# Hybrid SSD/RWKV block: gate and up with tokens on the output partitions

## The chip, the cores and the metric

The kernel runs on one core of a Trainium2 chip, in fp32. Matrix products are made of three float32r matmuls each (high part by high part, high by low, low by high), so that they come near to fp32. The metric is the device time of one execution in microseconds, the median of several runs.

## The reference

The block takes x, 256 tokens by 2048 channels. A normalised copy goes through one input projection into two mixers (a Mamba-2 state space mixer and an RWKV-7 time mixer), whose outputs go through w_out and are added to x. Then comes the feed-forward part, which the change touches, and a last norm:

```python
h = h + jnp.concatenate([y_ssd, y_rwkv], axis=-1) @ w_out[l]
v = rms_norm(h, norm2_g[l])
h = h + (jax.nn.silu(v @ w_gate[l]) * (v @ w_up[l])) @ w_down[l]
return rms_norm(h, norm_f_g)
```

w_gate and w_up are 2048 x 5632, w_down is 5632 x 2048, all fp32: 138 MB, read once.

## The kernel before

**Streamed weights.** Every weight matrix is read in units of 0.5 MB, in the order of use, on the queue of SyncE, into a ring of four buffers (raw). ScalarE casts a unit to its high part whi (L192), VectorE subtracts to get the low part wlo (L193); both have rings of four. TensorE consumes a unit with 24 matmuls of 256 columns or 12 of 512.

**Two forms of product.** gemm_a (L267) keeps a 128x128 piece of the weights stationary and moves the 256 tokens of one row tile of the activations: the output has channels on the partitions and tokens along the free dimension. A unit is four row tiles of 256 columns. gemm_b (L283) keeps 128 tokens of an activation tile stationary and moves 512 weight columns: the output has tokens on the partitions, in two tiles of one PSUM bank each (tokens 0 to 127, and 128 to 255). A unit is two row tiles of 512 columns. The input projection uses gemm_a, but for its z columns; z uses gemm_b (L1021), and so do w_out and w_down through add_out (L304), which adds the result to h. All product tiles come from a pool of four PSUM banks (mm), tiles for transposes and small work from another of four (mx).

**The second norm.** uh and ul (high and low part) hold h times the norm's weight with channels on the partitions, 16 row tiles. They are made by to_channels (L234) from PE transposes of h, a quarter of the channels after each quarter of the last w_out product. The rows' factor, one over the root mean square of each token, is left out there and comes in later: row_scale (L217) makes R, which holds it along the free dimension on every partition (a product of ones with a diagonal matrix), and scaled (L229) multiplies a product with it in PSUM, on VectorE.

**Feed-forward.** The loop (L1054) goes over 11 blocks of 512 feed-forward columns. In each, two halves of 256 columns have a gate and an up product by gemm_a (w_gate, silu on ScalarE, w_up, multiplication on VectorE), and the result is split into ah and al, with channels on the partitions, as the w_down product needs it. The w_down product of a block is traced after gate and up of the next block (prev). The last 256 rows of w_down are a piece of their own with the last norm, one half of the tokens after the other.

**Order.** The queues are in the order of the program but for small shifts that the scheduler of the language makes. side is a list of small pieces with due ticks; every unit of a product is one tick, and side.at(t, f) has f traced at the t-th tick from then. In the feed-forward part of the kernel before nothing is in it.

Of the kernel before, what the change touches and what calls it, by code (L numbers as in the profile page):

```python
# [10 lines left out]
F32 = mybir.dt.float32  # L11
# [20 lines left out]

# ticks of a window at which the parts of three pairs of blocks are traced
PREP = (1.081, 1.2, 4.2, 5.2, 5.536, 6.756, 8.05, 9.2)
# [7 lines left out]
class Side:  # L42
    """Work of the mixers, cut into small pieces that are traced between the pieces of the dense products."""

# [24 lines left out]
def tile_hybrid_block(ctx: ExitStack, tc: tile.TileContext, x, norm1_g, w_in, conv_w, conv_b, dt_bias, A_log, D_skip,  # L69
# [26 lines left out]

# [1 line left out]
    h = big.tile([P, 2, D], F32, name="h")  # L98
# [11 lines left out]
    eps6 = constcol(1e-6, "eps6")  # L110
    # products that nothing reads: the tensor engine has its full clock only after a busy stretch
    ps = mxt("ps_up")
# [31 lines left out]

# [1 line left out]
    trimask = const.tile([P, P], F32, name="trimask")  # L146
# [12 lines left out]
    for s in range(2):  # L159
        for hh in range(2):  # L160
            a = hh * 64
            nc.vector.tensor_tensor(sel[:, s, a + 32 * s:a + 32 * s + 32], ident[:, a:a + 32], ident[:, a + 32:a + 64],
                                    ALU.add)
    # msk16: lower off-diagonal blocks on the way from 16 to 32 ([t, c])
    bmask = const.tile([P, 4], F32, name="bmask")
# [21 lines left out]
    colC = const.tile([P, 96], F32, name="colC")  # L187
# [1 line left out]
    def split(raw, order=lambda ins: ins):  # L189
# [10 lines left out]
    def square(i, pool, b, n, eng, order=lambda ins: ins):  # L200
        """the sum of squares of a quarter of each row"""
        src = h[:, b, n * 512:(n + 1) * 512]
        acc = ssq[i][:, b, n:n + 1]
        if eng == "act":
            order(nc.scalar.activation(pool.tile([P, 512], F32, name="sq_a"), src, AF.Square, accum_out=acc))
        else:
            order(nc.vector.scalar_tensor_tensor(pool.tile([P, 512], F32, name="sq_v"), src, 1.0, src, ALU.mult,
                                                 ALU.mult, accum_out=acc))
# [8 lines left out]
    def row_scale(i, pool):  # L217
        """one over the root mean square of each token, along the free dimension of every partition"""
        nonlocal R
        ps = mxt("ps_R")  # L220
        for b in range(2):
            r = finish(i, b)
            dg = pool.tile([P, P], F32, name="diag_r")
            nc.vector.tensor_scalar(dg, ident, r, None, ALU.mult)
            nc.tensor.matmul(ps[:, b * P:(b + 1) * P], ones, dg, start=True, stop=True)
        R = const.tile([P, T], F32, name="R")
        nc.scalar.copy(R, ps[:, :T])

    def scaled(ps):  # L229
        """a product of the raw rows becomes the one of the normalised rows"""  # L230
        nc.vector.tensor_tensor(ps, ps, R.unsqueeze(1).broadcast_to([P, 2, T]), ALU.mult)
        return ps

    def to_channels(n, gcol, order=lambda ins: ins):  # L234
        """a quarter of h times the norm's weight, with channels on the partitions; the rows' scale comes later"""
        nonlocal uh, ul
        if n == 0:
            uh = big.tile([P, KT, T], F32R, name="uh")
            ul = big.tile([P, KT, T], F32R, name="ul")
        tiles = []  # L240
        for k2 in range(2):
            ps = mxt("ps_n").rearrange("p (a t) -> p a t", a=2)
            tiles.append(ps)
            for b in range(2):
                for j in range(2):
                    c = n * 512 + (2 * k2 + j) * P
                    order(nc.tensor.transpose(out=ps[:, j, b * P:(b + 1) * P], in_=h[:, b, c:c + P], identity=ident))

        def half(k2):
            ks = [(4 * n + 2 * k2 + j, tiles[k2][:, j]) for j in range(2)]  # L250
            for k, ps in ks:
                order(nc.scalar.activation(uh[:, k], ps, AF.Copy, scale=gcol[:, k:k + 1]))
            for k, ps in ks:
                order(nc.vector.scalar_tensor_tensor(ul[:, k], ps, gcol[:, k:k + 1], uh[:, k].bitcast(F32), ALU.mult,
                                                     ALU.subtract))

        return half

    def load_a(w, cols, k0):
        """four row tiles of 256 columns; cols: [(place, width, column)]"""  # L260
        raw = wpool.tile([P, 4, 256], F32, name="raw", tag="raw", bufs=4)
        wv = w.rearrange("(k p) c -> p k c", p=P)
        for at, n, c in cols:
            nc.sync.dma_start(out=raw[:, :, at:at + n], in_=wv[:, k0:k0 + 4, c:c + n])
        return raw
# [17 lines left out]
    def gemm_b(w, r0, c0, acts, name):  # L283
        """acts: [(hi, lo)] with [P, T] each, one for a row tile of w; 512 columns"""
        ps = [mmt(name).rearrange("p a t -> p (a t)") for _ in range(2)]
# [18 lines left out]
    def add_out(w, r0, ys, then=None):  # L304
        """ys: [(hi, lo)] of two row tiles each"""
        acts = [(yh[:, k], yl[:, k]) for yh, yl in ys for k in range(2)]
# [7 lines left out]

    # the first product starts while x and its weights still come in, a quarter of the channels after the other
    pin = tc.keep_in_program_order
# [62 lines left out]

# [1 line left out]
    dtb = ssdc.tile([P, 3, 32], F32, name="dtb")  # L381
# [50 lines left out]

# [1 line left out]
    yq = deque()  # L434
    NCH = 8

    def rwkv_pair(pi, st):
# [119 lines left out]
        def swap(dst, src, tmp):  # L557
            """the 64x64 blocks of src [(h c), (b c t)] transposed into dst [(h t), b c, c]"""
            fl = src.rearrange("p a t -> p (a t)")
# [35 lines left out]

        # inverse of (I - N): blocks of 16 on one partition each, by halves of halves
        def inv_out():
# [15 lines left out]
        def inv_level(s):  # L613
            def f():
# [3 lines left out]
                def blocks(t, at, swap):  # L618
                    """block (row offset or column offset) of each of the nm diagonal blocks, [nm, s, s]"""
                    v = t[:, :nm * 34 * s].rearrange("p (m x) -> p m x", m=nm)[:, :, at:at + 16 * s]  # L620
                    v = v.rearrange("p m (j t) -> p m j t", t=16)[:, :, :, 0:s]
                    return v.rearrange("p m j t -> p m t j") if swap else v

                # nb is [i, t]: N[t, i]; xb is [t, c]
                n21 = blocks(nb, s, False)
# [6 lines left out]
                tt = tl("tt", (64, 64), 2)  # L632
                # three free dimensions in an instruction: blocks of 2 by rows, larger ones by blocks
                if s == 2:
# [9 lines left out]
                def product(out, a, b):  # L644
                    """out[m, r, c] = sum over j of a[m, r, j] b[m, c, j]"""
                    for m, r in cut:
# [27 lines left out]
        def blocks32(out, lhs, rhs, rows):  # L674
            """out[:, c] = lhs[:, c].T @ rhs[:, c] for 32x32 blocks; rows: [(input rows, output rows)]"""
            for c in range(NCH):
# [47 lines left out]

        # the chunks in their order
        def step_r(c):
# [149 lines left out]

# [1 line left out]
    window(8, 20)  # L878
# [166 lines left out]

# [1 line left out]
    row_scale(1, npool)  # L1047
    npool.release()
    xzst.close()
    fp = ctx.enter_context(tc.tile_pool(name="fp", bufs=2))  # L1050
    gfb = fp.tile([P, D], F32, name="gfb", bufs=1)
    nc.gpsimd.dma_start(out=gfb, in_=norm_f_g.partition_broadcast(P))
    prev = None
    for j in range(D_FF // 512):  # L1054
        acts = []
        for i in range(2):
            c = j * 512 + i * 256
            ah = fp.tile([P, 2, T], F32R, name="ah", bufs=5)
            al = fp.tile([P, 2, T], F32R, name="al", bufs=5)
            acts.append((ah, al))  # L1060
            psg = scaled(gemm_a(w_gate, [(0, 256, c)], "ps_gt"))
            sg = fp.tile([P, 2, T], F32, name="sg")
            nc.scalar.activation(sg, psg, AF.Silu)
            psu = scaled(gemm_a(w_up, [(0, 256, c)], "ps_up"))
            nc.vector.tensor_tensor(sg, psu, sg, ALU.mult)
            nc.scalar.copy(ah, sg)
            nc.vector.tensor_tensor(al, sg, ah.bitcast(F32), ALU.subtract)
        if prev is not None:
            add_out(w_down, *prev)
        prev = (j * 512, acts)  # L1070
    add_out(w_down, prev[0], prev[1][:1])

    # the last 256 rows of w_down and the last norm, one half of the tokens after the other
    (yh, yl), r0 = prev[1][1], prev[0] + 256
# [64 lines left out]
```

## Time and profile before

| | |
|---|---|
| median of three runs | 1697.96 us (1697.33 to 1699.16) |
| profiled execution, span from first to last instruction | 1697.0 us |
| TensorE busy | 1678.6 us, 99% |
| VectorE, ScalarE busy | 1232.7 us, 892.1 us |
| feed-forward part, first gate matmul to the first of the last piece | 940.05 to 1676.92 us |
| HBM read | 282.27 MB, 169 GB/s over the span |

The profiler records every instruction of each engine with its start and duration. Durations of matmuls overlap (one of 256 columns is listed with 283 ns, yet the next starts after 120), so the rate of TensorE is read from the distance between starts. The page gives no time of the profiled execution beside its span; the runs' times lie about 1 us above it.

### The profile page before, as it was taken

What the parts mean: (1) busy time and instruction counts of PE and PEld (TensorE: products, weight loads), DVE (VectorE), ACT (ScalarE), POOL (GpSimd) and SP (SyncE); (2) the same over time, 40 slices, a digit from 0 to 9 for tenths busy, and PEclk for the clock granted to TensorE, in tenths of its full rate; (3) what the DMA queues carried; (4) which work ended last, traced back from release to release, by engine and by line L of the source; (5) the groups of instructions that cost most, each with busy time, mean ns of one, the idle gap of its engine ahead of it and who ended that gap; (6) DMA issues with size and microseconds to landing.
All of it is one profiled execution on the core that took longest, in us unless ns stands there. A gap on an engine that the chain in (4) does not pass through costs nothing.

```text
span 1697.0 us, 35291 instructions
## 1 busy us (share of the span) xinstructions
PE 1678.6 (99%) x14670; PEld 1546.5 (91%) x14670; DVE 1232.7 (73%) x1921; ACT 892.1 (53%) x1391; POOL 18.0 (1%) x57
## 2 busy tenths in 40 slices
PE   8999999999999999999999999999999999999997
PEld 8999989889898998998988999999999999999996
DVE  7998888989888868877768656556565565565657
ACT  6655665765646556666665543434434334344344
POOL 3000000000000000000000000000000000000000
PEclk9999999999999999999999999999999999999999
DMA  8554445544445456565554655555555555555553
GB/s 256 175 152 115 126 128 156 145 120 143 132 130 151 141 154 217 179 206 164 164 177 150 205 183 190 181 189 187 185 189 182 189 189 182 190 186 185 190 182 129
DMA packets 266720, 288.27 MB, mean 170 GB/s; under 512 B 43426, under 2 KB 216768, under 8 KB 265920
## 3 DMA queue, kind: packets, MB, share of 16 engines
q1 hardware_dynamic: 265232, 283.72, 54.0%
q8 instruction: 115, 1.88, 0.4%
q0 software_dynamic: 752, 1.24, 0.2%
q10 hardware_dynamic: 576, 1.05, 0.2%
q14 instruction: 45, 0.37, 0.1%
HBM read 282.27 MB, written 3.70 MB: 169 GB/s over the span
## 4 chain that ended last, share of the span: by engine, by line
PE 71%; DVE 2%; DMA 1%; ACT 1%; issue 0%; DVEq 0%
PE ps_o L298 7%; PE ps_o L300 7%; PE ps_o L299 7%; PE ps_up L279 5%; PE ps_up L277 5%; PE ps_up L278 5%; PE ps_gt L279 5%; PE ps_gt L278 5%; PE ps_gt L277 5%; PE ps_xs L277 2%; PE ps_xs L279 2%; PE ps_xs L278 2%; PE ps_z L300 2%; PE ps_z L298 2%; PE ps_z L299 2%; PE ps_bc L277 1%
## 5 line engine op out<-in xcount | busy, mean ns | idle before, releaser
L192 ACT CAST whi<-raw 128x1024 fp32r<-128x1024 f32 x508 | 532.2, 1048 | 655.2 <-PE ps_o L300 144.8
L193 DVE TENSOR_TENSOR wlo<-raw,whi 128x1024 fp32r<-128x1024 f32 x508 | 619.7, 1220 | 335.2 <-ACT whi L192 333.4
L277 PE MATMUL ps_rkv<-uh,whi 128*128 128x256 f32 x768 | 224.7, 293 | 0.0
L279 PE MATMUL ps_rkv<-uh,wlo 128*128 128x256 f32 x768 | 218.3, 284 | 0.7 <-DVE wlo L193 0.7
L278 PE MATMUL ps_rkv<-ul,whi 128*128 128x256 f32 x768 | 218.3, 284 | 0.0
L278 PE MATMUL ps_gt<-ul,whi 128*128 128x256 f32 x704 | 199.4, 283 | 0.0
L279 PE MATMUL ps_gt<-uh,wlo 128*128 128x256 f32 x704 | 199.3, 283 | 0.0
L277 PE MATMUL ps_up<-uh,whi 128*128 128x256 f32 x704 | 199.2, 283 | 0.0
L278 PE MATMUL ps_up<-ul,whi 128*128 128x256 f32 x704 | 199.2, 283 | 0.0
L279 PE MATMUL ps_up<-uh,wlo 128*128 128x256 f32 x704 | 199.2, 283 | 0.0
L277 PE MATMUL ps_gt<-uh,whi 128*128 128x256 f32 x704 | 199.2, 283 | 0.0
L277 PEld LDWEIGHTS ps_rkv<-uh,whi 128*128 128x128 f32 x768 | 146.7, 191 | 5.5 <-issue 1.4
L279 PEld LDWEIGHTS ps_rkv<-uh,wlo 128*128 128x128 f32 x768 | 146.7, 191 | 1.9 <-DVE wlo L193 1.1
L278 PEld LDWEIGHTS ps_rkv<-ul,whi 128*128 128x128 f32 x768 | 146.8, 191 | 0.6
L278 PEld LDWEIGHTS ps_gt<-ul,whi 128*128 128x128 f32 x704 | 135.1, 192 | 0.4
L277 PEld LDWEIGHTS ps_gt<-uh,whi 128*128 128x128 f32 x704 | 135.1, 192 | 0.4
L277 PEld LDWEIGHTS ps_up<-uh,whi 128*128 128x128 f32 x704 | 135.2, 192 | 0.0
L278 PEld LDWEIGHTS ps_up<-ul,whi 128*128 128x128 f32 x704 | 135.2, 192 | 0.0
L279 PEld LDWEIGHTS ps_up<-uh,wlo 128*128 128x128 f32 x704 | 135.2, 192 | 0.0
L279 PEld LDWEIGHTS ps_gt<-uh,wlo 128*128 128x128 f32 x704 | 135.1, 192 | 0.0
L298 PE MATMUL ps_o<-whi,ah 128*128 128x512 f32 x336 | 130.8, 389 | 0.0
L299 PE MATMUL ps_o<-wlo,ah 128*128 128x512 f32 x336 | 130.8, 389 | 0.0
(338 smaller groups left out, 3272.0 us busy)
## 6 DMA issues: line engine op xcount, KB each, us to landing
raw<-in_w_in_dram SPq DMA_DIRECT2D x180, 512.0 KB, 3.9
raw<-in_w_gate_dram SPq DMA_DIRECT2D x88, 512.0 KB, 3.6
raw<-in_w_up_dram SPq DMA_DIRECT2D x88, 512.0 KB, 3.5
raw<-in_w_down_dram SPq DMA_DIRECT2D x88, 512.0 KB, 3.6
raw<-in_w_out_dram SPq DMA_DIRECT2D x64, 512.0 KB, 3.9
csb<-cs_d SPq DMA_DIRECT2D x4, 1024.0 KB, 5.7
h<-in_x_dram SPq DMA_DIRECT2D x4, 512.0 KB, 7.8
g2s<-in_rwkv_g_dram SPq DMA_DIRECT2D x8, 256.0 KB, 3.3
```

What stands on the lines that cost most here:

```text
L192: order(nc.scalar.copy(hi, raw))
L193: order(nc.vector.tensor_tensor(lo, raw, hi.bitcast(F32), ALU.subtract))
L277: nc.tensor.matmul(o, wh, uh[:, kt], start=first and b == 0, stop=False)
L278: nc.tensor.matmul(o, wh, ul[:, kt], start=False, stop=False)
L279: nc.tensor.matmul(o, wl, uh[:, kt], start=False, stop=last and b == 1)
L298: nc.tensor.matmul(ps[b], ah[:, s], hi[:, k], start=first, stop=False)
L299: nc.tensor.matmul(ps[b], ah[:, s], lo[:, k], start=False, stop=False)
L300: nc.tensor.matmul(ps[b], al[:, s], hi[:, k], start=False, stop=last)
```

## The change

Gate and up are made by gemm_b: uh and ul stationary, 512 weight columns moving, 16 row tiles in eight units. The products have tokens on the partitions, so the rows' factor is a value per partition: it goes into silu as its scale, and into the multiplication of up and silu as a scalar operand (r1). The result gt, [128 tokens, 2, 512 columns], is turned back to channels by eight PE transposes (two PSUM tiles of four) in back, which is due 1.5 ticks later, and split from PSUM into ah and al. R, its product and the scaling passes are not made for this norm. ah and al are rings of two tiles of 512 columns instead of five of 256.

```diff
-    row_scale(1, npool)
+    r1 = [finish(1, b) for b in range(2)]
...
+    uacts = [(uh[:, k], ul[:, k]) for k in range(KT)]
+
+    def back(gt, ah, al):
+        def f():
+            for b in range(2):
+                ps = mxt("ps_t").rearrange("p (k t) -> p k t", k=4)
+                for k in range(4):
+                    nc.tensor.transpose(out=ps[:, k], in_=gt[:, b, k * P:(k + 1) * P], identity=ident)
+                s = slice(b * P, (b + 1) * P)
+                nc.scalar.copy(ah[:, :, s], ps)
+                nc.vector.tensor_tensor(al[:, :, s], ps, ah[:, :, s].bitcast(F32), ALU.subtract)
+        return f
+
     prev = None
     for j in range(D_FF // 512):
-        acts = []
-        for i in range(2):
-            c = j * 512 + i * 256
-            ah = fp.tile([P, 2, T], F32R, name="ah", bufs=5)
-            al = fp.tile([P, 2, T], F32R, name="al", bufs=5)
-            acts.append((ah, al))
-            psg = scaled(gemm_a(w_gate, [(0, 256, c)], "ps_gt"))
-            sg = fp.tile([P, 2, T], F32, name="sg")
-            nc.scalar.activation(sg, psg, AF.Silu)
-            psu = scaled(gemm_a(w_up, [(0, 256, c)], "ps_up"))
-            nc.vector.tensor_tensor(sg, psu, sg, ALU.mult)
-            nc.scalar.copy(ah, sg)
-            nc.vector.tensor_tensor(al, sg, ah.bitcast(F32), ALU.subtract)
+        c = j * 512
+        ah = fp.tile([P, 4, T], F32R, name="ah")
+        al = fp.tile([P, 4, T], F32R, name="al")
+        sg = fp.tile([P, 2, 512], F32, name="sg", bufs=1)
+        gt = fp.tile([P, 2, 512], F32, name="gt", bufs=1)
+        for b, ps in enumerate(gemm_b(w_gate, 0, c, uacts, "ps_gt")):
+            nc.scalar.activation(sg[:, b], ps, AF.Silu, scale=r1[b])
+        for b, ps in enumerate(gemm_b(w_up, 0, c, uacts, "ps_up")):
+            nc.vector.scalar_tensor_tensor(gt[:, b], ps, r1[b], sg[:, b], ALU.mult, ALU.mult)
+        side.at(1.5, back(gt, ah, al))
         if prev is not None:
-            add_out(w_down, *prev)
-        prev = (j * 512, acts)
+            add_out(w_down, prev[0], prev[1])
+        prev = (c, [(ah[:, :2], al[:, :2]), (ah[:, 2:], al[:, 2:])])
+    side.drain()
```

Three places show how the queues change. The first is TensorE's queue inside a gate product; the numbers behind the names tell tiles of one name apart. Before, the last matmuls of one unit of weights and the first of the next (the second operand is the stationary one, uh and ul move):

```order
L277 MATMUL ps_gt_13249<-uh_11853,whi_13252 128x256
L278 MATMUL ps_gt_13249<-ul_11854,whi_13252 128x256
L279 MATMUL ps_gt_13249<-uh_11853,wlo_13253 128x256
L277 MATMUL ps_gt_13249<-uh_11853,whi_13282 128x256
L278 MATMUL ps_gt_13249<-ul_11854,whi_13282 128x256
```

Of the change, one row tile of weights, moving past both halves of the tokens:

```order
L298 MATMUL ps_gt_12378<-whi_12400,uh_11853 128x512
L299 MATMUL ps_gt_12378<-wlo_12401,uh_11853 128x512
L300 MATMUL ps_gt_12378<-whi_12400,ul_11854 128x512
L298 MATMUL ps_gt_12379<-whi_12400,uh_11853 128x512
L299 MATMUL ps_gt_12379<-wlo_12401,uh_11853 128x512
L300 MATMUL ps_gt_12379<-whi_12400,ul_11854 128x512
```

The operands have changed sides, each matmul has twice the columns, and two output tiles take turns.

The second place is TensorE's queue where the w_down product goes from its first 512 output columns to the next (two units into the product). Before:

```order
L298 MATMUL ps_o_13088<-whi_13109,ah_12334 128x512
L299 MATMUL ps_o_13088<-wlo_13110,ah_12334 128x512
L300 MATMUL ps_o_13088<-whi_13109,al_12335 128x512
L298 MATMUL ps_o_13127<-whi_13131,ah_12083 128x512
L299 MATMUL ps_o_13127<-wlo_13132,ah_12083 128x512
```

Of the change:

```order
L299 MATMUL ps_o_12689<-wlo_12711,ah_12074 128x512
L300 MATMUL ps_o_12689<-whi_12710,al_12075 128x512
L1061 MATMUL ps_t_12726<-ident_73,gt_12377 128x128 x4
L1061 MATMUL ps_t_12733<-ident_73,gt_12377 128x128 x4
L298 MATMUL ps_o_12742<-whi_12746,ah_12074 128x512
L299 MATMUL ps_o_12742<-wlo_12747,ah_12074 128x512
```

The eight transposes of the block's gt stand between the two; w_down itself works on the ah and al of the block before.

The third place is VectorE's queue from the last units of up into the w_down product. Before:

```order
L193 TENSOR_TENSOR wlo<-raw,whi 128x1024 x4
L231 TENSOR_TENSOR ps_up<-ps_up,R 128x512
L1065 TENSOR_TENSOR sg<-ps_up,sg 128x512
L193 TENSOR_TENSOR wlo<-raw,whi 128x1024
L1067 TENSOR_TENSOR al<-sg,ah 128x512
L193 TENSOR_TENSOR wlo<-raw,whi 128x1024
L311 TENSOR_TENSOR h<-ps_o,h 128x512 x2
```

Of the change:

```order
L193 TENSOR_TENSOR wlo<-raw,whi 128x1024 x13
L1077 SCALAR_TENSOR_TENSOR gt<-ps_up,rstd_168,sg 128x512 x2
L193 TENSOR_TENSOR wlo<-raw,whi 128x1024 x2
L311 TENSOR_TENSOR h<-ps_o,h 128x512 x2
L193 TENSOR_TENSOR wlo<-raw,whi 128x1024
L1064 TENSOR_TENSOR al<-ps_t,ah 128x4x128 x2
```

The scaling and the multiplication have become one pass per half of the tokens at the same place, and the low part al is made later, from PSUM, behind the first additions to h. In the kernel before the same pieces also stand in the middle of the block, for its first 256 columns.

## Rows read from the trace of the kernel before

**Rows 1.** The profile page: busy time by engine, and the granted clock by slice.
```profile
PE 1678.6 (99%) x14670; PEld 1546.5 (91%) x14670; DVE 1232.7 (73%) x1921; ACT 892.1 (53%) x1391; POOL 18.0 (1%) x57
...
PEclk9999999999999999999999999999999999999999
```

**Rows 2.** Busy time by stage: PE, PEld, DVE, ACT, POOL; clock; DMA share, GB/s.
```profile
799.00:811.00 12.00, 12.00 (x55) 9.93 (x54) 5.92 (x5) 5.46 (x6) 0.00 (x0) 1.00 0.69 207
...
935.70:937.10 1.40, 1.40 (x12) 1.24 (x11) 1.40 (x3) 0.56 (x3) 0.00 (x0) 1.00 0.42 148
...
1055.30:1101.37 46.07, 46.07 (x385) 46.07 (x384) 23.90 (x23) 18.38 (x19) 0.00 (x0) 1.00 0.57 183
1101.37:1123.16 21.79, 21.79 (x98) 18.03 (x97) 15.51 (x18) 9.05 (x9) 0.00 (x0) 1.00 0.59 192
```

**Rows 3.** Timeline of PE in block 2: start, duration, line, operation.
```profile
1055.30 0.28 PE L277 MATMUL ps_gt<-uh,whi 128*128 128x256 f32 x1
...
1101.37 0.40 PE L298 MATMUL ps_o<-whi,ah 128*128 128x512 f32 x1
...
1102.30 0.39 PE L299 MATMUL ps_o<-wlo,ah 128*128 128x512 f32 x1
...
1123.16 0.28 PE L277 MATMUL ps_gt<-uh,whi 128*128 128x256 f32 x1
```

**Rows 4.** Timeline of PE in one z product.
```profile
799.85 0.39 PE L298 MATMUL ps_z<-whi,uh 128*128 128x512 f32 x1
...
811.19 0.39 PE L300 MATMUL ps_z<-whi,ul 128*128 128x512 f32 x1
```

**Rows 5.** Timeline of PE around eight transposes of the second norm.
```profile
935.73 0.40 PE L298 MATMUL ps_o<-whi,yh 128*128 128x512 f32 x1
...
935.96 1.04 PE L247 MATMUL ps_n<-ident,h 128*128 128x128 f32 x8
...
936.75 0.47 PE L299 MATMUL ps_o<-wlo,yh 128*128 128x512 f32 x1
...
937.07 0.39 PE L300 MATMUL ps_o<-whi,yl 128*128 128x512 f32 x1
```

**Rows 6.** Timeline of PE around the row scale of the second norm.
```profile
947.51 0.61 PE L225 MATMUL ps_R<-diag_r,ones 128*128 128x128 f32 x4
947.88 0.36 PE L278 MATMUL ps_gt<-ul,whi 128*128 128x256 f32 x1
948.08 0.28 PE L279 MATMUL ps_gt<-uh,wlo 128*128 128x256 f32 x1
```

**Rows 7.** Groups by line and form: busy, mean ns, idle before; z by tile.
```profile
L192 ACT CAST whi<-raw 128x1024 fp32r<-128x1024 f32 x257 | 269.7, 1049 | 416.5 <-PE ps_gt L278 142.3 <-PE ps_o L300 122.3 <-PE ps_up L278 119.7
L193 DVE TENSOR_TENSOR wlo<-raw,whi 128x1024 fp32r<-128x1024 f32 x258 | 315.8, 1224 | 273.5 <-ACT whi L192 273.5
L231 DVE TENSOR_TENSOR ps_up<-ps_up,R 128x512 f32<-128x512 f32 x22 | 15.4, 700 | 14.4 <-PE ps_up L279 14.4
L1109 DVE SCALAR_TENSOR_TENSOR hg<-h,rstd,gfb 128x512 f32<-128x512 f32 x2 | 1.4, 742 | 0.0
...
L1024 ACT ACTIVATE zs<-ps_z,rstd x8: 680/684/691, 673.5 to 886.1; 128x512 f32<-128x512 f32 x8
```

**Rows 8.** Waits over the whole run: us in total, times, longest.
```profile
ACT whi L192 <- PE ps_gt L278: 142.3, 86, 1.8
...
ACT whi L192 <- DMA raw<-in_w_in_dram: 3.8, 6, 1.8
```

**Rows 9.** Timeline of PE, ACT and DVE at the end of up in block 1.
```profile
1033.39 0.28 PE L279 MATMUL ps_up<-uh,wlo 128*128 128x256 f32 x1
...
1033.59 1.05 ACT L192 CAST whi<-raw 128x1024 fp32r<-128x1024 f32 x1 [1.79 <-PE ps_up L278]
...
1033.71 0.70 DVE L231 TENSOR_TENSOR ps_up<-ps_up,R 128x512 f32<-128x512 f32 x1 [0.65 <-PE ps_up L279]
```

**Rows 10.** DMA issues of gate's weights: count, size, median us to landing.
```profile
raw<-in_w_gate_dram SPq DMA_DIRECT2D x88, 512.0 KB, 3.6
```

## The prediction

> **What bounds the kernel now.** I read the engine shares first [rows 1]: TensorE is busy for 1678.6 of 1697.0 us, 99%, and the granted clock is at its upper level (2.4 GHz) in all 40 slices. Busy says little by itself, so the second view is busy time by stage [rows 2]. In the gate and up products (1055.30 to 1101.37) and in the w_down product behind them (1101.37 to 1123.16) TensorE is busy for the whole stretch, while VectorE has 23.90 + 15.51 = 39.4 us and ScalarE 18.38 + 9.05 = 27.4 us of work in 67.86 us. So in the feed-forward part a microsecond less on TensorE's queue is a microsecond less in the span, as long as the split weights keep coming. The third view is the waits [rows 8]: ScalarE's casts wait for TensorE to free a buffer (142.3 us behind gate alone), but for loaded weights only 3.8 us in the whole run. Feeding is ahead, TensorE sets the pace.
>
> Since matmul durations overlap, I cost by the distance between starts [rows 3]. From the first gate matmul at 1055.30 to the first w_down matmul at 1101.37 there are 384 matmuls of 256 columns: 46.07 us, 120.0 ns each. From there to the next gate at 1123.16 there are 96 of 512 columns: 21.79 us, 227.0 ns each. Two narrow ones take 240 ns, one wide one 227 ns, for the same arithmetic. The z product of the state space mixer uses the very operands that the change will use (slices of uh and ul stationary, split weights moving, 512 columns, eight units of two row tiles): its starts at 799.85 and 811.19 stand 50 matmuls apart [rows 4], 226.8 ns each, with no gap between units and tokens on the output partitions.
>
> **Removed and added, step by step.** Per block of 512 feed-forward columns.
>
> Products: 384 x 120.0 ns = 46.07 us become 192 x 226.8 ns = 43.55 us, 2.52 us less; 11 blocks give 27.7 us. Bounds of the new price: the best is the steady spacing inside a product, 0.68 us for three, 226.7 ns (28.0 us less). The worst is that of the first matmuls of w_down, 1101.37 to 1102.30, four in 0.93 us, 232.5 ns [rows 3]; if all of gate and up ran like that, a block would take 44.64 us and the gain would be 15.7 us. I take 226.8, because the z product is the same instruction on the same operands and runs through 11 us at it.
>
> Transposes: eight per block, 88 in all, fp32, of one 128x128 piece each. The same form stands in the norm's turn to channels between w_out matmuls [rows 5]. A matmul starts at 935.73, eight transposes begin at 935.96, the next matmul is at 936.75 and the one after it at 937.07. Two matmuls should take 0.45 us of these 1.34 us; the eight cost 0.89 us, and this includes the slow restart (0.32 us instead of 0.23). 11 x 0.89 = 9.8 us. The lower bound is their own stretch alone, 0.79 us, 8.7 us in all. Less than that is excluded, since TensorE has no idle time in which to put them. The clock stays at its upper level in that stretch [rows 2]. The Trainium skill ("TensorE: Matmul & The Clock Gate", Part 4: PE-mode transpose) gives about 275 ns for a 128x128 transpose in one kernel's context; that would be an estimated 24.2 us, and 4 us of gain in all. The 0.11 us here is a spacing in a stream, with each one's latency hidden behind the next.
>
> Row scale: the ones-by-diagonal product of the second norm goes. Its four records begin at 947.51, and the matmuls behind it start at 947.88 and 948.08 [rows 6]; without it they would start at 947.51 and 947.63, so 0.45 us is saved. The scale moves into silu's per-partition scale and the up eviction.
>
> Edits costed at nothing on the path. ScalarE: two silus of 128x512 with a per-partition scale as in the z product (684 ns [rows 7]) and two casts from PSUM, the same number as before. VectorE: eight passes of 128x512 at about 0.70 us become four, two of them scalar_tensor_tensor (742 ns) [rows 7]. Both have less or equal work in a block that is some 1.6 us shorter; their cover is the 40% or more of each block in which they idle. Loads: a unit is still 0.5 MB, but its matmuls last 12 x 0.2268 = 2.72 instead of 24 x 0.120 = 2.88 us. The w_down stretch already runs on such units at 192 GB/s, and the z product at 207 [rows 2], both without a TensorE gap.
>
> Waits that the change adds, with what is queued behind them. (1) VectorE's gt waits for the end of up, as the scaling of up does now. In before the last up matmul starts at 1033.39 and VectorE begins at 1033.71 [rows 9], 0.32 us later. The first half ends three matmuls earlier (0.68 us), so gt is done about 0.32 + 0.74 = 1.1 to 1.5 us after the last up matmul starts. The split behind it is that of a unit three ahead, as now: ScalarE's cast at 1033.59 is released by the buffer of four units before. (2) The transposes wait for gt on TensorE's queue, with the whole w_down product behind them. They stand after two units of it, 5.4 us after up's end, so about 4 us of margin; for the first block they stand after two units of the next gate. (3) ah on ScalarE waits for the transposes, with the cast for unit seven of w_down behind it. That cast can't start before unit three is through, 2.7 us later, while the two ah take 1.2 us. (4) PSUM: each product now takes two of the four banks at once. w_down's first two are gate's, read 20 us before; its next two are up's, free by gt and wanted after 5.4 us.
>
> Sum: -27.7 + 9.8 - 0.45 = -18.4 us. The profiled span of 1697.0 becomes 1678.6; the median of the runs, 1697.96, lies 0.96 us above that span, so I add this back: 1679.6 us. What lies ahead of the feed-forward part and the last norm keep their instructions and order.
>
> **Rivals.**
> (a) Wide matmuls gain nothing in gate and up: their spacing rises to that of two narrow ones while other engines read PSUM and write the split weights. Break-even is where 2112 x (240.0 - x) equals 9.3 us: 235.6 ns. For it: the 232.5 ns at the start of w_down. Against it: the z product with the same traffic. If the gain were 5 us, the time would be 1697.96 - 5.3 + 9.3 = 1702, slower. Chance 0.03. The Trainium skill (the same page, Back-to-back issue gap) has N/2.4 + 2.5 ns, thus 109.2 and 215.8 ns, from which one wide for two narrow saves an estimated 5.3 us in 2112. The trace disagrees: 120.0 and 226.8, some 13 ns of fixed cost per matmul.
> (b) TensorE waits at the transposes because gt is late (VectorE held by a split or an addition). Price: the wait itself, once a block; above 18.4 / 11 = 1.7 us per block the kernel is slower. It takes a gt 5.7 us later than reckoned; VectorE's queue has at most one split (1.22 us) in front of it. With 2.5 us a block: 1707. Chance 0.02.
> (c) Feeding falls behind at the shorter unit: a wait at each of the 176 units of gate and up. 0.1 us a unit eats the gain. A cast and a subtraction take 1.05 and 1.22 us of 2.72 [rows 7], on two engines; a load lands in 3.6 us [rows 10], with four buffers. A part of it, 0.03 us a unit, would give 1685. Chance 0.05, of which 0.01 for no gain.
> (d) Transposes dearer than in the norm, since each block starts them behind a wait on another engine's semaphore and reads gt from VectorE's newest writes: at 0.25 us each 22 us, 1692. Chance 0.04.
> (e) The forecast, 0.86.
>
> **How the numbers follow.** A measurement of this kernel can tell about 0.2%, 3.4 us, from no change. Faster: (e), most of (c) and (d), 0.93. Same: 0.03, from the edges of (a), (c) and (d). Slower: 0.04 from (a) and (b). Low: the best spacing and the cheapest transposes give 28.0 - 8.7 + 0.45 = 19.8, 1678.2, and 1 us of scatter as in the three runs, thus 1677. High: (c) and half of the way to the worst spacing (21.7 - 9.8 + 0.45 = 12.4, 1685.6), thus 1687.
>
> **What would show it.** In the profile of the changed kernel a block of gate and up should last 43.5 to 43.6 us with TensorE busy throughout, the eight ps_t transposes 0.8 us with one slow matmul behind them, w_down with them 22.7 us, a whole block 66.2 instead of 67.9. ScalarE's casts should still wait for TensorE and not for loads. I am wrong if TensorE idles before ps_t (b), if it waits for wlo or whi at units (c), if spacing in gate is above 230 ns (a), or if the granted clock falls around the transposes.

## The result and the profile after

The changed kernel takes 1681.24 us (median of four runs, 1677.68 to 1683.16) against 1697.86 (four runs, 1697.33 to 1699.16) on the same chip: a ratio of 0.990, 95% interval 0.9886 to 0.9914, 16.6 us less. The forecast was 1679.6 in a range of 1677 to 1687. The profiled execution has a span of 1676.0 us, of which the feed-forward part (first gate matmul to the first matmul of the last piece) is 718.15 (937.62 to 1655.77); before it was 736.87 (940.05 to 1676.92). So 18.72 us come from there, where 18.4 were forecast, and 2.3 us from outside. In the tiles of the changed kernel (the last two numbers ahead of the semicolon are the first and the last start of a kind):

```profile
L298 PE MATMUL ps_gt<-whi,uh x352: 389/389/478, 937.6 to 1599.8; 128*128 128x512 f32 x176
...
L1103 PE MATMUL ps_f<-dhi,ah x16: 389/389/389, 1655.8 to 1666.0; 128*128 128x512 f32 x16
```

The page, engines and clock by slice, to set against [rows 1]:

```profile
PE 1658.2 (99%) x12642; PEld 1443.7 (86%) x12642; DVE 1203.2 (72%) x1875; ACT 892.8 (53%) x1390; POOL 17.9 (1%) x57
...
PEclk9999999999999999999999999999999999999999
```

TensorE is still busy 99% of the span at the upper clock, with 2,028 matmuls fewer: it remains the bound, and the gain is less work on its queue. Busy time by stage, gate and up of block 2 and then its w_down product (PE, PEld, DVE, ACT, POOL; clock; DMA share, GB/s), answering [rows 2]:

```profile
1049.16:1092.68 43.52, 43.52 (x193) 36.05 (x192) 20.80 (x19) 18.13 (x18) 0.00 (x0) 1.00 0.64 193
1092.68:1115.37 22.69, 22.69 (x106) 18.85 (x104) 15.92 (x19) 9.41 (x10) 0.00 (x0) 1.00 0.63 188
```

Gate and up last 43.52 us instead of 46.07, w_down with the transposes 22.69 instead of 21.79: a block 66.21 instead of 67.86. VectorE does 36.7 us in it (39.4 before), ScalarE 27.5 (27.4), so neither comes near. The same places in the timeline of PE (start, duration, line, operation), answering [rows 3] and [rows 5]:

```profile
1049.16 0.39 PE L298 MATMUL ps_gt<-whi,uh 128*128 128x512 f32 x1
...
1092.68 0.39 PE L298 MATMUL ps_o<-whi,ah 128*128 128x512 f32 x1
...
1097.89 0.40 PE L300 MATMUL ps_o<-whi,al 128*128 128x512 f32 x1
1098.13 1.04 PE L1061 MATMUL ps_t<-ident,gt 128*128 128x128 f32 x8
1098.92 0.47 PE L298 MATMUL ps_o<-whi,ah 128*128 128x512 f32 x1
1099.23 0.39 PE L299 MATMUL ps_o<-wlo,ah 128*128 128x512 f32 x1
...
1115.37 0.39 PE L298 MATMUL ps_gt<-whi,uh 128*128 128x512 f32 x1
```

From 1049.16 to 1092.68 there are 192 wide matmuls, 226.7 ns each. The eight transposes start as soon as the matmul ahead of them has been issued (0.23 us, the usual distance), with no wait for gt, and the next matmul stands 0.79 us later, the one behind it 0.31. The tiles of the turn by operation (duration min, median, max):

```profile
L1061 PE MATMUL ps_t<-ident,gt x88: 270/273/273, 987.5 to 1628.4; 128*128 128x128 f32 x88
L1063 ACT CAST ah<-ps_t x22: 578/586/592, 988.7 to 1629.3; 128x512 fp32r<-128x512 f32 x22
L1064 DVE TENSOR_TENSOR al<-ps_t,ah x22: 679/683/686, 989.9 to 1630.7; 128x512 fp32r<-128x512 f32 x22
...
L1077 DVE SCALAR_TENSOR_TENSOR gt<-ps_up,rstd,sg x22: 741/744/746, 981.8 to 1622.6; 128x512 f32<-128x512 f32 x22
```

The reckoning of gt shows in the timeline of VectorE and ScalarE at the end of up:

```profile
1092.39 1.40 DVE L1077 SCALAR_TENSOR_TENSOR gt<-ps_up,rstd,sg 128x512 f32<-128x512 f32 x2
1092.88 1.06 ACT L192 CAST whi<-raw 128x1024 fp32r<-128x1024 f32 x1 [1.67 <-PE ps_up L300]
1093.97 1.23 DVE L193 TENSOR_TENSOR wlo<-raw,whi 128x1024 fp32r<-128x1024 f32 x1 [0.17 <-ACT whi L192]
```

The last up matmul starts at 1092.45 and both halves of gt are through at 1093.79, 1.34 us later; the transposes come at 1098.13. The split behind it, for a unit that is three ahead, waits 0.17 us for ScalarE's cast and not for gt. ScalarE's casts wait for TensorE as before, to set against [rows 8]:

```profile
ACT whi L192 <- PE ps_gt L300: 124.8, 75, 1.7
```

### The profile page after: what moved, and what is told of

The parts are those of the page before. It is cut to its first block, busy times and chain, and to the rows that moved or that the text cites. A ratio compares the mean times of both kernels' runs of the same rounds, so it can differ in the third digit from the quotient of the medians.

```text
span 1676.0 us, 31111 instructions
## 1 busy us (share of the span) xinstructions
PE 1658.2 (99%) x12642; PEld 1443.7 (86%) x12642; DVE 1203.2 (72%) x1875; ACT 892.8 (53%) x1390; POOL 17.9 (1%) x57
## 4 chain that ended last, share of the span: by engine, by line
PE 75%; DVE 2%; DMA 1%; ACT 0%; issue 0%; DVEq 0%
PE ps_o L298 8%; PE ps_o L300 8%; PE ps_o L299 8%; PE ps_gt L298 5%; PE ps_up L298 5%; PE ps_gt L300 5%; PE ps_gt L299 5%; PE ps_up L299 5%; PE ps_up L300 5%; PE ps_xs L277 2%; PE ps_xs L279 2%; PE ps_xs L278 2%; PE ps_z L298 2%; PE ps_z L300 2%; PE ps_z L299 2%; PE ps_rkv L277 1%
## 5 line engine op out<-in xcount | busy, mean ns | idle before, releaser
L298 PE MATMUL ps_gt<-whi,uh 128*128 128x512 f32 x352 | 137.1, 390 | 0.0
L299 PE MATMUL ps_gt<-wlo,uh 128*128 128x512 f32 x352 | 137.0, 389 | 0.0
L300 PE MATMUL ps_gt<-whi,ul 128*128 128x512 f32 x352 | 137.0, 389 | 0.0
L298 PE MATMUL ps_up<-whi,uh 128*128 128x512 f32 x352 | 136.9, 389 | 0.0
L299 PE MATMUL ps_up<-wlo,uh 128*128 128x512 f32 x352 | 136.9, 389 | 0.0
L300 PE MATMUL ps_up<-whi,ul 128*128 128x512 f32 x352 | 136.9, 389 | 0.0
L300 PE MATMUL ps_o<-whi,al 128*128 128x512 f32 x336 | 130.9, 390 | 0.0
L311 DVE TENSOR_TENSOR h<-ps_o,h 128x512 f32<-128x512 f32 x184 | 120.5, 683 | 3.0 <-PE ps_o L300 2.6
L298 PE MATMUL ps_o<-whi,yh 128*128 128x512 f32 x256 | 104.6, 413 | 0.0
L300 PE MATMUL ps_o<-whi,yl 128*128 128x512 f32 x256 | 101.2, 396 | 0.0
```

The source lines that it names most:

```text
L298: nc.tensor.matmul(ps[b], ah[:, s], hi[:, k], start=first, stop=False)
L299: nc.tensor.matmul(ps[b], ah[:, s], lo[:, k], start=False, stop=False)
L300: nc.tensor.matmul(ps[b], al[:, s], hi[:, k], start=False, stop=last)
L311: nc.vector.tensor_tensor(d, ps[b], d, ALU.add)
```

## The experiments

My theory: in the feed-forward part only the spacing of instructions on TensorE's queue counts; wide matmuls take 2.55 us less a block, and eight transposes give 0.89 of it back. The rivals: part of the gain is from evictions and scaling that went, the transposes cost more than their own stretch or are partly hidden, or the difference is scatter between executions. Lengths of the feed-forward part are distances between starts in each trace, as above.

**The changed kernel again.**

> The changed kernel once more, as the base of this set and to tell where its runs differ. By my theory the feed-forward part (first gate matmul to the first matmul of the last piece) lasts 718.1 us as in its first profile (736.9 before), whatever the whole takes; the spread of its runs, 1677.7 to 1683.2, lies in the part ahead of the feed-forward part, whose instructions are the same in both kernels and which was 2.2 us shorter in the first profile of the changed kernel. A rival: the feed-forward part itself varies, by some 5 us, and the gain of 18.7 us in the first profile was a lucky one. Median by the theory 1677 to 1683, and a feed-forward part within 1 us of 718.1.

Median 1680.53 us against 1699.04 before: ratio 0.9893 (0.9878 to 0.9908). The feed-forward part took 718.11 us, within 0.04 of the first profile. The part ahead of it was 1.1 us longer than in that profile (938.69 against 937.62 us), and there it had been 2.4 us shorter than before, not the 2.2 of the expectation. So in the two profiles what the change touches is constant to a hundredth of a per cent, and the scatter is ahead of it (its place: last section). The theory stands and the rival falls for these two; the runs that were only timed have no stages to look at.

**Without the turn.**

> The eight transposes of each block are left out: ah and al are cast straight from gt, so what w_down gets is in the wrong places, and the time is that of the kernel without the turn. By my theory the turn costs 0.89 us a block on TensorE and nothing else: 9.8 us less than the changed kernel, a feed-forward part of 708.4 us, and 27 to 28 us less than before. Rival: the turn costs more than its own stretch (a wait for gt, w_down slower behind it, dearer evictions), then clearly more than 9.8 us go. Other rival: it is hidden, then the time stays.

```diff
-                ps = mxt("ps_t").rearrange("p (k t) -> p k t", k=4)
-                for k in range(4):
-                    nc.tensor.transpose(out=ps[:, k], in_=gt[:, b, k * P:(k + 1) * P], identity=ident)
+                ps = gt[:, b].rearrange("p (k t) -> p k t", k=4)
```

1670.58 us against 1699.04 before. First gate matmul and first matmul of the last piece:

```profile
L298 PE MATMUL ps_gt<-whi,uh x352: 389/389/478, 939.7 to 1592.7; 128*128 128x512 f32 x176
...
L1101 PE MATMUL ps_f<-dhi,ah x16: 389/389/389, 1647.8 to 1658.0; 128*128 128x512 f32 x16
```

The feed-forward part is 708.12 us, 10.0 less than with the turn (9.8 expected), 0.91 a block. Both rivals fall: the turn is not hidden, and it costs TensorE what its place on the queue said, to 0.02 us a block.

**The turn twice.**

> Each transpose is made twice into the same place (16 a block), so the result stands. By my theory each costs its spacing of about 0.1 us and the slow restart is paid once: 8 x 0.1 = 0.79 us more a block, 8.7 us in all over the changed kernel, a feed-forward part of about 726.8 us. If bursts of transposes let the granted clock fall, or hold up the stream of weight loads, more than that: over 12 us.

```diff
-                for k in range(4):
+                for k in (0, 1, 2, 3, 0, 1, 2, 3):
```

1690.51 us, feed-forward part 727.75: 9.6 us more than the changed kernel, where I expected 8.7. The first block's turn in the timeline of PE:

```profile
990.50 0.40 PE L300 MATMUL ps_gt<-whi,ul 128*128 128x512 f32 x1
990.73 1.91 PE L1061 MATMUL ps_t<-ident,gt 128*128 128x128 f32 x16
992.40 0.47 PE L298 MATMUL ps_gt<-whi,uh 128*128 128x512 f32 x1
992.71 0.39 PE L299 MATMUL ps_gt<-wlo,uh 128*128 128x512 f32 x1
```

Sixteen take 1.67 us from first start to the next matmul, eight took 0.79. Eight more are 0.88 us, so each costs 0.11. Single records of both traces start 0.109 us apart. Behind the last transpose the next matmul starts after only 0.03 us, and the one behind it stands 0.31 instead of 0.23 us away: the two deviations cancel, and the "slow restart" is no charge of its own. The 0.89 a burst was right; its split into 0.10 each and a restart was not, and 0.79 is no lower bound. The granted clock is 1.00 from 990 to 995 us, around this burst, too; the case with over 12 us did not come.

**The new layout with narrow matmuls.**

> Gate and up in the layout of the change, with its evictions and transposes, but each matmul moves 256 columns instead of 512, and there are twice as many. By my theory the whole gain comes from the spacing of matmuls (240 ns for two of 256, 226.8 for one of 512), so a block of gate and up takes 46.07 us again and the kernel takes 27.7 us more than the changed one, about 9 us more than before. Rival: part of the gain comes from what else the change removes (scaling passes, waits at the ends of the products); then the time stays below the one of before.

```diff
-                    nc.tensor.matmul(ps[b], ah[:, s], hi[:, k], start=first, stop=False)
...
+                    for q in range(cut):
+                        m = slice(q * 512 // cut, (q + 1) * 512 // cut)
+                        o = ps[b][:, m]
+                        nc.tensor.matmul(o, ah[:, s], hi[:, k, m], start=first and q == 0, stop=False)
...
-        for b, ps in enumerate(gemm_b(w_gate, 0, c, uacts, "ps_gt")):
+        for b, ps in enumerate(gemm_b(w_gate, 0, c, uacts, "ps_gt", 2)):
```

The two matmuls left out of this cut change in the same way, and up gets the 2 as gate does.

1707.78 us against 1699.04 before: ratio 1.0055 (1.004 to 1.007), slower by half a per cent.

```profile
L301 PE MATMUL ps_gt<-whi,uh x704: 277/283/363, 940.8 to 1630.2; 128*128 128x256 f32 x176
...
L1106 PE MATMUL ps_f<-dhi,ah x16: 389/389/389, 1687.2 to 1697.4; 128*128 128x512 f32 x16
```

The feed-forward part is 746.39 us, 28.2 more than with wide matmuls (27.7 expected) and 9.5 more than before; gate and up of a block last 46.07 us again. With the width undone nothing is left of the gain: the 9.5 us are the turn's 10.0 less half a microsecond, about what the row scale was put at. Layout, evictions and scaling passes show nothing else on the path.

**Three widths in one kernel.**

> As the changed kernel, but in blocks 2, 3 and 4 gate and up move 256 columns a matmul, and in blocks 6, 7 and 8 they move 128 (four matmuls in place of one); the other blocks move 512. It is read by blocks. If each matmul has a fixed cost of some 13 ns beside its columns (512 columns 226.8 ns, 256 columns 120.0), one of 128 columns takes 53 + 13 = 67 ns and gate and up of a block take 768 x 67 ns = 51 us, against 43.5 and 46.1 for the wider ones. The rival: the narrow spacing is that of the weight load that every matmul has ahead of it (the weight loads were busy 46.07 of 46.07 us in a narrow block and 18.03 of 21.79 in a wide one), and 120 ns is its floor; then 128 columns take 120 ns too, and a block takes 92 us.

```diff
-        for b, ps in enumerate(gemm_b(w_gate, 0, c, uacts, "ps_gt", 2)):
+        for b, ps in enumerate(gemm_b(w_gate, 0, c, uacts, "ps_gt", (2 if j in (2, 3, 4) else 4 if j in (6, 7, 8) else 1))):
```

The same for up. The one run took 1814.92 us. Gate and up of blocks 2 (256 columns), 5 (512) and 6 (128), columns as in the stages above:

```profile
1051.79:1097.86 46.07, 46.07 (x386) 46.03 (x385) 20.97 (x19) 18.02 (x18) 0.00 (x0) 1.00 0.58 184
1258.12:1301.64 43.52, 43.52 (x194) 36.04 (x193) 20.80 (x19) 18.13 (x18) 0.00 (x0) 1.00 0.60 192
1324.29:1410.00 85.71, 85.71 (x770) 85.67 (x768) 21.44 (x19) 18.02 (x18) 0.00 (x0) 1.00 0.32 105
```

46.07, 43.52 and 85.71 us for 384, 192 and 768 matmuls: 120.0, 226.7 and 111.6 ns each, all at clock 1.00. Both expectations missed the last. From 256 to 512 columns the spacing grows by 106.7 ns, which is 256 columns at 2.4 GHz, and 13.3 ns are left over at either width: there it is columns plus a fixed cost. At 128 that would be 67 ns, but the spacing stays at 111.6, where the weight loads are busy for 85.67 of 85.71 us: a floor, which I had put at 120. That the weight loads set it is likely but not shown, since they are busy throughout at 256 columns, too. The narrow matmuls of before ran 8 ns above this floor, so the gain of the change is not the floor but the fixed 13.3 ns of 2,112 matmuls (28.1 us). Every matmul here has a weight load of its own, so whether the 13.3 ns belong to the matmul or to the load that goes with it stays open.

**The turn at once.**

> As the changed kernel, but the transposes of a block are traced right behind up, ahead of the w_down product, so that they stand on TensorE's queue two matmuls into it instead of two units (0.5 instead of 5.4 us after up's end). By my theory gt is done about 1.1 to 1.5 us after up's end, so TensorE now waits some 0.7 to 1.1 us for it in each of 11 blocks: 8 to 12 us more than the changed kernel, and the profile shows the wait at ps_t on VectorE. If the wait is shorter than 0.2 us a block, the place of the transposes did not matter and the margin was reckoned wrongly; with 1.7 us or more the gain of the change would be gone.

```diff
-        side.at(1.5, back(gt, ah, al))
+        back(gt, ah, al)()
```

1679.31 us, as fast as the changed kernel; feed-forward part 719.33, 1.2 us longer and not 8 to 12. The idle time ahead of ps_t (us, times; it is that of TensorE's weight loads), and the timeline of TensorE, its weight loads (PEld) and VectorE around it:

```profile
  DVE gt L1077: 3.5, 11
```

```profile
1025.59 1.41 DVE L1077 SCALAR_TENSOR_TENSOR gt<-ps_up,rstd,sg 128x512 f32<-128x512 f32 x2
1025.65 0.39 PE L300 MATMUL ps_up<-whi,ul 128*128 128x512 f32 x1
...
1026.39 0.42 PEld L1061 LDWEIGHTS ps_t<-ident,gt 128*128 128x128 f32 x4 [0.32 <-DVE gt L1077]
1026.39 0.66 PE L1061 MATMUL ps_t<-ident,gt 128*128 128x128 f32 x4
...
1026.80 0.48 PE L300 MATMUL ps_o<-whi,al 128*128 128x512 f32 x1
1027.05 0.43 PEld L1061 LDWEIGHTS ps_t<-ident,gt 128*128 128x128 f32 x4
...
1027.12 0.60 PE L1061 MATMUL ps_t<-ident,gt 128*128 128x128 f32 x4
```

The expectation missed: it forgot that the turn is two halves. The first four transposes need only the first half of gt, which is ready 0.7 us after the last up matmul starts, and the scheduler put a matmul between the halves. In every block the first weight load of either half starts 0.05 us after its half of gt is done, so both halves wait for gt, but shortly: the weight loads idle for 0.32 and 0.08 us. The matmuls already on the way cover most of it, and 0.1 us a block is left in the feed-forward part. The margin of 4 us in the prediction was real, and all but 0.1 us of it was not needed.

**The turn off TensorE.** The experiments say that TensorE's queue is all that counts and that 9 us of it are transposes, while VectorE, ScalarE and the DMA engines have room.

> As the changed kernel, but ten of the eleven turns leave TensorE: VectorE transposes gt in blocks of 32 by 32 (two instructions of 128x512), and one write to device memory and four reads, issued by ScalarE's queue, bring the blocks to their partitions; the last block keeps its transposes on TensorE. By my theory TensorE alone sets the pace of the feed-forward part, VectorE and ScalarE have over 40% of it idle, and the loads have room (4096 pieces of 128 bytes at 13 ns on one of 16 engines are some 3.3 us of 66 a block), so ten turns of 0.89 us go: 9 us less than the changed kernel, a feed-forward part of 709.1 us, some 1671 us in all. Rival: the waits on ScalarE's queue, the extra work of VectorE or the extra transfers hold up the split weights, TensorE waits for wlo or whi, and less than 5 us is left of it, or it is slower.

```diff
+    def by_dma(gt, tr, ah, al):
+        for b in range(2):
+            nc.vector.transpose(tr[:, b], gt[:, b])
+        gd = dram.tile([T, 512], F32, name="gd")
+        st = {}
+        def write():
+            nc.scalar.dma_start(out=gd.rearrange("(b p) f -> p b f", p=P), in_=tr)
+        def read():
+            st["g"] = fp.tile([P, 4, T], F32, name="gc", bufs=1)
+            dv = gd.rearrange("(a j) (k q i) -> q j k a i", j=32, q=4, i=32)
+            for q in range(4):
+                nc.scalar.dma_start(out=st["g"][32 * q:32 * q + 32].rearrange("j k (a i) -> j k a i", i=32), in_=dv[q])
+        def cut():
+            nc.scalar.copy(ah, st["g"])
+            nc.vector.tensor_tensor(al, st["g"], ah.bitcast(F32), ALU.subtract)
+        side.at(4.5, write)
+        side.at(6.5, read)
+        side.at(11.5, cut)
...
-        side.at(1.5, back(gt, ah, al))
+        if j < D_FF // 512 - 1:
+            by_dma(gt, sg, ah, al)
+        else:
+            side.at(1.5, back(gt, ah, al))
```

1669.41 us against 1696.53 before: ratio 0.9843 (0.9828 to 0.9857), 27 us less. The changed kernel was not run beside it; its own ratio to before was 0.9893. The feed-forward part is 709.05 us, where 709.1 was expected, and 9.1 less than that of the changed kernel:

```profile
L298 PE MATMUL ps_gt<-whi,uh x352: 389/389/478, 936.6 to 1589.7; 128*128 128x512 f32 x176
...
L1130 PE MATMUL ps_f<-dhi,ah x16: 389/389/389, 1645.7 to 1655.9; 128*128 128x512 f32 x16
```

From the page, the transfers of ScalarE's queue (packets, MB, share of 16 engines) and the issues (count, size, median us to landing), then a wait:

```profile
q10 hardware_dynamic: 44896, 11.54, 3.1%
```

```profile
raw<-in_w_gate_dram SPq DMA_DIRECT2D x88, 512.0 KB, 4.4
...
gd<-sg ACTq DMA_DIRECT2D x10, 512.0 KB, 4.6
gc<-gd ACTq DMA_DIRECT2D x40, 128.0 KB, 6.4
```

```profile
ACT whi L192 <- PE ps_gt L300: 114.4, 71, 1.7
```

The price of a piece was right: packets of 128 bytes take a median of 13 ns in the traces of before and of this run. Weights land in 4.4 us instead of 3.7, and ScalarE's casts still wait for TensorE. The turn has left the path. The rival (queues or transfers hold up the split weights) falls. Of the versions that compute the block's result it is the fastest that was run.

## Why the prediction was right

**The products.** Forecast 43.55 us a block, measured 43.52. The spacing was read from the z product, the same instruction on the same operands; rival (a), the spacing at the start of w_down, did not come, and narrow_moves shows that this term carries the whole gain but for half a microsecond, to which the row scale's 0.45 fits.

**The transposes.** Forecast 0.89 us a block; w_down takes 22.65 to 22.69 us with them and 21.76 without. no_turn and double_turn give 10.0 and 9.6 us for 88. The price was read rightly as a whole, but its lower bound of 8.7 us took the 0.79 us of a burst as its own stretch; a burst costs eight times 0.11. Rival (d), a dearer turn behind a semaphore, falls: no wait stands before ps_t.

**Edits costed at nothing.** Loads, casts and subtractions stayed hidden (c), and gt was ready as reckoned (1.34 us against 1.1 to 1.5), so (b) falls too; turn_now shows that a short wait for gt costs less than its length.

**The sum.** 18.72 us in the feed-forward part against 18.4. What the sum had not foreseen lies outside: I took the part ahead as unchanged in time because its instructions and order are, and it was 2.4 us shorter in the profile; and I added 0.96 us for what lies around the span, where the profiled execution of the changed kernel has 1.68 (1677.68 to 1676.0). The median of the four runs lies 1.6 us above the forecast; that it came so close is in part luck, since the part ahead alone scatters by more than that. Those runs' spans go from 1676.0 to 1681.5; which part of them that is, the timed runs don't show.

**The rule for the spacing.** The Trainium skill ("TensorE: Matmul & The Clock Gate", Back-to-back issue gap) gives columns over 2.4 plus 2.5 ns for the gap of an isolated matmul. The prediction took it for the spacing in this stream in rival (a), where it makes the change lose an estimated 4 us (5.3 gained, 9.3 paid). The trace disagrees: the part that doesn't depend on columns is 13.3 ns at 256 and at 512 columns here, where a weight load goes with each matmul.

## What to carry to other kernels

Where TensorE's queue is full, read the distance between starts, not the durations, and look for the same instruction elsewhere in the same trace: one stage gave the new price to 0.1%, another that of the transposes. A product that could have either operand stationary was cheaper here with the wide one moving, by the fixed cost of each matmul saved (13.3 ns); the turn of layout on the same queue ate over a third of that, and was worth moving to engines that idle. Halves of a tile that are waited for apart can make a wait much shorter than the chain ahead of it (0.1 us a block instead of 0.7 to 1.1).

## What the runs showed of the hardware

Two things. A matmul of 128 columns is no cheaper than 111.6 ns in a stream where each loads its weights, little less than one of 256 (120.0), and a transpose in a burst costs about the same, 110 ns.

And the part ahead of the feed-forward part, the same program in every kernel here (VectorE and ScalarE have the same instructions in the same order), differs by up to 4.2 us between profiles (the first gate matmul is at 936.6 us in turn_by_dma and at 940.8 in double_turn). In `before`, double_turn and narrow_moves, over half of the distance to the earliest, turn_by_dma, comes from one place in the RWKV stage: from one split of a weight unit (421.4 us in the changed kernel) to the sixth after it these three take 30.0 to 30.2 us, the changed kernel and turn_by_dma 27.8. Windows of 5 us there (columns as in the stages), before:

```profile
440.00:445.00 5.00, 3.39 (x101) 2.37 (x89) 3.38 (x8) 4.00 (x11) 0.00 (x0) 0.90 0.46 130
445.00:450.00 5.00, 5.00 (x48) 4.19 (x48) 3.04 (x7) 4.90 (x12) 0.00 (x0) 0.76 0.00 0
```

and after:

```profile
440.00:445.00 5.00, 4.29 (x109) 3.39 (x98) 4.38 (x10) 4.86 (x13) 0.00 (x0) 1.00 0.50 138
445.00:450.00 5.00, 5.00 (x24) 4.20 (x23) 4.55 (x9) 4.90 (x12) 0.00 (x0) 1.00 0.02 4
```

Before, TensorE idles 1.61 us of the first window and the granted clock falls to a mean of 0.90 and 0.76; after, it idles 0.71 and the clock stays at 1.00. The nines of the page's clock row (90% or more of a slice) don't show this, so "the upper level in all 40 slices" in the prediction holds for the feed-forward part but not here. double_turn fell as before (1.67 us idle, 0.93 and 0.73), and so did narrow_moves (1.69, 0.77 and 0.88); no_turn did not (1.77 us idle, 1.00 in both), so the length of this idle time alone doesn't decide it. What makes the idle time differ was not tried.
